# Half-depth block products in the up projection, and a down projection with the depth as its outer loop

## The chip, the core and the metric

The kernel runs on one core of one Trainium2 chip. The metric is device time in microseconds from the first to the last instruction of one execution, in float32. TensorE (PE) multiplies a 128x128 stationary block with up to 512 moving columns and adds up in PSUM, which has eight banks of 128x512 float32 here; VectorE (DVE), ScalarE (ACT) and GpSimd (POOL) do the elementwise work on PSUM and SBUF (POOL on SBUF alone); every DMA is issued from SyncE's queue (SP).

## What is computed

One layer of a hybrid decoder: a token mixer, a cross-attention and a gated ConvFFN, each between two RMS norms and added to the residual. Only the ConvFFN and its last norm change:

```python
def conv_ffn(h, w_up, conv_w, conv_b, w_down):      # h (1024, 1024), w_up (1024, 5632), w_down (2816, 1024)
    a = causal_depthwise_conv(h @ w_up, conv_w, conv_b)   # output t reads t-2, t-1, t
    val, gate = jnp.split(a, 2, axis=-1)
    return (val * jax.nn.gelu(gate)) @ w_down

h = rmsnorm(x, g_ffn_pre)
x = x + rmsnorm(conv_ffn(h, ...), g_ffn_post)
```

## The kernel before

**Numbers.** Every float32 operand of a large product is held as a pair: `hi`, rounded by an ACT copy to the format that PE takes at full rate, and `lo`, the rest, from a DVE subtraction (`split`, L213 and L214). `mm3` (L193 to L195) makes a product of three matmuls for each 128-deep step: hi*hi, hi*lo, lo*hi.

**Layout.** Activations stand transposed: channels in partitions, tokens in the free axis, in two halves `h` of 512 tokens. The 5632 up channels are 44 blocks of 128; block i and block i+22 are the value and the gate of pair i, so there are 22 pairs. `xg[h][k]` is the input of half h in depth step k (of 8).

**Weights.** `Stream` (L53) holds one list of weight tiles of 128x512 in the order of use. A tile is loaded (SP, into one of 4 `raw` slots), split by ACT (L95) and DVE (L98; some tiles in `ON_POOL` go to POOL), and kept as a pair in 13 `w` slots. `pump`, called by `tick` once or twice in a product, keeps the splits `W_AHEAD` = 6 tiles ahead of use. `tick` also moves on the `sides`: generators such as `post` and `finish`, whose instructions are woven into the products.

**ConvFFN.** `up_block(i, q, h)` is one block of one half: 8 depth steps, 24 matmuls of 512 columns, two weight tiles. Then the convolution: ACT writes tap 2 and the bias (L1174), DVE adds the two shifted taps (L1177, L1178), and two short DVE operations carry the edge from half 0 to half 1 (L1181, L1182). For a gate, ACT applies GELU (L1186), POOL multiplies (L1188), and the product is split into `f_hl`. The first `LEAD` = 5 pairs are done for all of half 0 and then for all of half 1, since half 1's input comes from `post2[1]`, the norms after attention, which runs beside half 0's blocks (L684 to L707) and is emitted to its end before half 1's blocks begin.

**Down.** The 22 pairs are in six groups (`GROUPS`). After the first pair of a group, `down` of the group before it takes eight output blocks and both halves: 3 or 4 depth steps a product, evicted and added on DVE to 16 `ya` tiles (L1207). The last group is done in `quarters` for half 1: twice eight products of 256 columns, with the end norm of the first 256 tokens beside the products of the second.

**Order.** A planner (`schedule_with_timeline_sim=True`) simulates the program when it is built and lays down the order of each engine's instructions; at run time each engine takes its own in that order, waiting on semaphores. `pin` keeps the order as written (used in the second quarter).

Of the kernel before, what the change touches and what calls it, by code (L numbers as in the profile page):

```python
# [22 lines left out]
P = 128  # L23
# [8 lines left out]
GROUPS = (4, 4, 4, 3, 3, 4)  # L32
LEAD = 5
FILL = 3
B_FIRST = 1

W_AHEAD = 6
ON_POOL = ((4, 16, 1), (164, 184, 2))
# [8 lines left out]
TAIL_R = 1  # L47
TAIL_B = 3
# [4 lines left out]
SLOTS_3 = {"f": 19, "t": 6, "rs": 4}  # L53
BANKS = {"acc": 4, "sx": 3, "st": 1}
DOWN = [(h, 0, 512, b) for b in range(8) for h in range(2)]
LAST_A = [(0, 0, 512, b) for b in range(8)]


class Stream:
# [13 lines left out]
    def add(self, ap):  # L73
        self.items.append(ap)
        return len(self.items) - 1

    def load_to(self, n):
        n = min(n, len(self.items), self.done + SLOTS["raw"])
        while self.loaded < n:
            ap = self.items[self.loaded]  # L80
            t = self.k.slot("raw")
            w = ap.shape[1] * ap.shape[2]
            self.k.nc.sync.dma_start(t[:, :w].rearrange("p (a b) -> p a b", b=ap.shape[2]), ap)
            self.raw[self.loaded] = (t, w)
            self.loaded += 1

    def split_to(self, n):
        nc = self.k.nc
        n = min(n, len(self.items))
        while self.done < n:  # L90
            self.load_to(self.done + 1)
            i = self.done
            t, w = self.raw.pop(i)
            hi, lo = self.k.pair(self.tag.get(i, "w"))
            nc.scalar.copy(hi[:, :w], t[:, :w])  # L95
            eng = "g" if any(a <= i < b and i % m == 0 for a, b, m in ON_POOL) else "v"
            e = nc.vector if eng == "v" else nc.gpsimd
            e.tensor_tensor(lo[:, :w], t[:, :w], hi[:, :w], ALU.subtract)  # L98
            self.hl[i] = (hi, lo)
            self.done += 1  # L100
            self.load_to(self.done + SLOTS["raw"])

    def pump(self, limit=1):
        self.split_to(min(self.pos + self.ahead, self.done + limit))
        self.load_to(self.done + SLOTS["raw"])
# [7 lines left out]
class Builder:  # L113
# [74 lines left out]
    def mm3(self, ps, parts, ticks=2, first=True, last=True):  # L188
# [3 lines left out]
        for i, (lh, ll, rh, rl) in enumerate(parts):  # L192
            self.pin(nc.tensor.matmul(ps, lhsT=lh, rhs=rh, start=first and i == 0, stop=False))  # L193
            self.pin(nc.tensor.matmul(ps, lhsT=lh, rhs=rl, start=False, stop=False))  # L194
            self.pin(nc.tensor.matmul(ps, lhsT=ll, rhs=rh, start=False, stop=last and i == n - 1))  # L195
# [518 lines left out]
    def finish(self, m, acc, h, x2d):  # L714
# [3 lines left out]
        for i in range(KT):  # L718
            t = self.slot("f")
# [20 lines left out]
    def run(self):  # L740
        with ExitStack() as es:
# [15 lines left out]
            self.shut(p)  # L757

    def prepare(self, cp, dp):
# [23 lines left out]
        self.pairs = []  # L783
        p0 = 0
        for n in GROUPS:
            self.pairs.append(list(range(p0, p0 + n)))
            p0 += n
        ids["up"], ids["dn"] = {}, {}
        for h in range(2):
            for i in range(LEAD):  # L790
                for q in range(2):
                    ids["up"][i, q, h] = add("w_up", i + 22 * q)
        for gi, gp in enumerate(self.pairs):
            for j, i in enumerate(gp):
                if i >= LEAD:
                    for q in range(2):
                        ids["up"][i, q, 0] = ids["up"][i, q, 1] = add("w_up", i + 22 * q)
                if j == 0 and gi:
                    self.add_down(gi - 1)
        for j, i in enumerate(gp):  # L800
            for q in range(2):
                ids["up"][i, q, 1] = add("w_up", i + 22 * q)
            if j == B_FIRST - 1:
                self.add_down(gi)
# [34 lines left out]
        self.x2d = halves("x2d", 8)  # L839
        self.xg = [[], []]  # L840
# [3 lines left out]

    def add_down(self, gi):
        k0, n = self.pairs[gi][0], len(self.pairs[gi])
        for b in range(8):
            i = self.ids["dn"][gi, b] = self.w.add(self.a["w_down"][b][:, k0:k0 + n])
            if gi == len(self.pairs) - 1:
                self.w.tag[i] = "b"  # L850
# [164 lines left out]
    def attention(self):  # L1015
# [108 lines left out]
        m2 = [[None] * 8, [None] * 8]  # L1124
# [32 lines left out]

    def ffn(self):
        nc, w, ids, pairs = self.nc, self.w, self.ids, self.pairs
        v, g = nc.vector, nc.gpsimd  # L1160
        conv = self.conv
        nc.sync.dma_start(conv, self.a["conv"])
        edge = self.tiny([P, 44, 2], "edge", 1)
        self.side(self.post2[1], POST_2B)
        val, f_hl, ya = {}, {}, {}

        def up_block(i, q, h):
            blk = i + 22 * q
# [3 lines left out]
            t = self.slot("t")  # L1172
            cw = lambda j: conv[:, blk, j:j + 1]
            nc.scalar.activation(t, ps, AF.Identity, bias=cw(3), scale=cw(2))  # L1174
            if h == 0:
                nc.scalar.copy(edge[:, blk], ps[:, 510:512])  # L1176
            v.scalar_tensor_tensor(t[:, 1:512], ps[:, 0:511], cw(1), t[:, 1:512], ALU.mult, ALU.add)  # L1177
            v.scalar_tensor_tensor(t[:, 2:512], ps[:, 0:510], cw(0), t[:, 2:512], ALU.mult, ALU.add)  # L1178
            if h == 1:
                hl = edge[:, blk]  # L1180
                v.scalar_tensor_tensor(t[:, 0:1], hl[:, 1:2], cw(1), t[:, 0:1], ALU.mult, ALU.add)  # L1181
                v.scalar_tensor_tensor(t[:, 0:2], hl[:, 0:2], cw(0), t[:, 0:2], ALU.mult, ALU.add)  # L1182
            if q == 0:
                val[i, h] = t
                return
            nc.scalar.activation(t, t, AF.Gelu_apprx_tanh)  # L1186
            f = val.pop((i, h))
            g.tensor_tensor(f, f, t, ALU.mult)  # L1188
            hl = f_hl[i, h] = self.pair("f")
            self.split(*hl, f)  # L1190

        def down(gi, sections=DOWN):
            gp = pairs[gi]
            n = len(gp)
            last = gi == len(pairs) - 1
            for h, c0, c1, b in sections:
                c = slice(c0, c1)
                hi, lo = w.get(ids["dn"][gi, b])
                ps = self.bank()[:, :c1 - c0]
                self.mm3(ps, [(hi[:, P * j:P * j + P], lo[:, P * j:P * j + P], *(t[:, c] for t in f_hl[gp[j], h]))  # L1200
                              for j in range(n)], ticks=1)
                if gi == 0:
                    ya[b, h] = self.slot("m")
                    nc.scalar.copy(ya[b, h], ps)
                    continue
                t = ya[b, h][:, c]
                v.tensor_tensor(t, t, ps, ALU.add)  # L1207
                if last:
                    if b == 0:
                        sq = self.slot("ac")  # L1210
                    self.sumsq(t, sq, b == 0)
                    if b == 7:
                        self.side(self.finish([ya[i, h] for i in range(8)], sq, h, self.x2d), 1)

        def quarters(gi):

            gp = pairs[gi]
            n = len(gp)
            wide = lambda x: x[:, :256].unsqueeze(1).to_broadcast([P, 2, 256])
            prev = None  # L1220

            def add(x):
                acc, sq, e = x
                self.pin(e.tensor_tensor(acc, acc, sq, ALU.add))

            for c0 in (0, 256):
                c = slice(c0, c0 + 256)
                self.pinned = c0 > 0
                acc = self.slot("ac")[:, :256]
                mg, res = [], []  # L1230
                steps = iter(())
                for b in range(8):
                    hi, lo = w.get(ids["dn"][gi, b])
                    ps = self.bank()[:, :256]
                    self.mm3(ps, [(hi[:, P * j:P * j + P], lo[:, P * j:P * j + P], *(t[:, c] for t in f_hl[gp[j], 1]))
                                  for j in range(n)], ticks=0)
                    if b % 2 == 0:
                        mg.append(self.slot("rs" if c0 else "t", shape=[P, 2, 256]))
                        res.append(self.slot("f", shape=[P, 2, 256]))
                    nc.sync.dma_start(res[-1][:, b % 2], self.x2d[b][1][:, c])  # L1240
                    t = ya[b, 1][:, c]
                    self.pin(v.tensor_tensor(t, t, ps, ALU.add))
                    sq = acc if b == 0 else self.slot("sq")[:, :256]
                    nc.scalar.activation(sq, t, AF.Square)
                    if b > 1:
                        add(late)
                    late = acc, sq, g if c0 == 0 and b < 6 else v
                    nc.scalar.activation(mg[-1][:, b % 2], t, AF.Identity, scale=self.gain["g_ffn_post"][:, b:b + 1])
                    if prev:
                        if b == TAIL_R:  # L1250
                            r = self.rms(prev[0], 2)
                        if b == TAIL_B:
# [119 lines left out]
```

## Time and profile before

| | |
|---|---|
| median of 3 runs | 1438.21 us (1436.39 to 1438.9) |
| the profiled execution, its time | 1437.53 us |
| its span, first to last instruction | 1435.8 us |
| mean granted TensorE clock | 0.972 |
| instructions | 18623, of which 6712 matmuls |
| DMA | 144.38 MB, 33.4% of 16 engines' span |

The page of the profile gives each engine's busy time and the mean duration of each group of instructions. Matmuls overlap: the duration of one is longer than the distance to the next, so what one more or less is worth is read from the distance of their starts in the timeline. Row counts of the matmuls may lack a few per cent.

### The profile page before, as it was taken

What the parts mean: (1) busy time and instruction counts of PE and PEld (TensorE: products, weight loads), DVE (VectorE), ACT (ScalarE), POOL (GpSimd) and SP (SyncE); (2) the same over time, 40 slices, a digit from 0 to 9 for tenths busy, and PEclk for the clock granted to TensorE, in tenths of its full rate; (3) what the DMA queues carried; (4) which work ended last, traced back from release to release, by engine and by line L of the source; (5) the groups of instructions that cost most, each with busy time, mean ns of one, the idle gap of its engine ahead of it and who ended that gap; (6) DMA issues with size and microseconds to landing.
All of it is one profiled execution on the core that took longest, in us unless ns stands there. A gap on an engine that the chain in (4) does not pass through costs nothing.

```text
span 1435.8 us, 18623 instructions
## 1 busy us (share of the span) xinstructions
PE 1361.4 (95%) x6712; PEld 1150.9 (80%) x6712; DVE 879.1 (61%) x1532; ACT 545.7 (38%) x1032; POOL 397.3 (28%) x336
## 2 busy tenths in 40 slices
PE   9799898799989998899989999999999999999996
PEld 7689887688868886788778888888888888888885
DVE  7968798874485558856787424444443454455576
ACT  7224321355454444445354423322331231324433
POOL 1675526832280027304641001000110010100313
PEclk9899999799999999999989999999999999999998
DMA  9653335264262135523424211111111112123441
GB/s 319 181 155 106 87 101 149 82 204 139 89 197 75 52 97 168 161 66 99 127 91 117 74 45 52 44 52 52 45 52 47 43 44 59 42 62 110 140 139 60
DMA packets 102268, 144.38 MB, mean 101 GB/s; under 512 B 28320, under 2 KB 39712, under 8 KB 102176
## 3 DMA queue, kind: packets, MB, share of 16 engines
q1 hardware_dynamic: 102176, 143.19, 33.4%
q8 instruction: 53, 0.87, 0.3%
q14 instruction: 39, 0.32, 0.1%
HBM read 119.71 MB, written 19.25 MB: 97 GB/s over the span
## 4 chain that ended last, share of the span: by engine, by line
PE 71%; DVE 13%; DMA 5%; issue 5%; POOL 4%; ACT 1%; SPq 1%; DVEq 0%; POOLq 0%; ACTq 0%
PE acc L194 22%; PE acc L195 22%; PE acc L193 22%; DVE w L98 2%; POOL ac L671 1%; DMA raw<-in_w_q 1%; DVE m L684 1%; DMA rs<-in_xT 1%; PE st L266 1%; PE sx L195 1%; DMA x<-x 1%; PE sx L193 1%; DVE x L558 1%; PE sx L194 1%; PE st L239 1%
## 5 line engine op out<-in xcount | busy, mean ns | idle before, releaser
L194 PE MATMUL acc<-b,w 128*128 128x512 f32 x1200 | 472.5, 394 | 7.3 <-DVE b L691 4.4
L193 PE MATMUL acc<-b,w 128*128 128x512 f32 x1200 | 473.0, 395 | 2.2 <-DVE t L1178 2.2
L195 PE MATMUL acc<-b,w 128*128 128x512 f32 x1200 | 471.8, 393 | 1.2 <-DVE w L98 1.2
L98 DVE TENSOR_TENSOR w<-raw,w 128x512 fp32r<-128x512 f32 (+1 forms) x302 | 249.5, 831 | 272.8 <-PE acc L194 201.0
L95 ACT CAST w<-raw 128x512 fp32r<-128x512 f32 (+1 forms) x324 | 198.7, 615 | 307.2 <-PE acc L195 248.5
L194 PEld LDWEIGHTS acc<-b,w 128*128 128x128 f32 x1200 | 228.3, 190 | 56.4 <-DVE b L691 6.3
L193 PEld LDWEIGHTS acc<-b,w 128*128 128x128 f32 x1200 | 228.3, 190 | 49.5 <-issue 2.8
L195 PEld LDWEIGHTS acc<-b,w 128*128 128x128 f32 x1200 | 227.7, 190 | 49.7 <-DVE w L98 2.7
L1188 POOL TENSOR_TENSOR t<-t,t 128x512 f32<-128x512 f32 x44 | 57.2, 1300 | 584.1 <-ACT t L1186 579.5
L671 POOL TENSOR_TENSOR ac<-ac,sq 128x512 f32<-128x512 f32 x49 | 72.2, 1482 | 192.3 <-ACT sq L670 148.5
L1177 DVE SCALAR_TENSOR_TENSOR t<-acc,conv,t 128x511 f32<-128x511 f32 x88 | 65.8, 748 | 85.7 <-ACT edge L1176 76.9
L1174 ACT ACTIVATE t<-acc,conv 128x512 f32<-128x512 f32 x88 | 68.5, 778 | 125.5 <-PE acc L195 125.4
L193 PE MATMUL acc<-f,w 128*128 128x512 f32 x288 | 112.0, 389 | 0.0
L194 PE MATMUL acc<-f,w 128*128 128x512 f32 x288 | 112.0, 389 | 0.0
L195 PE MATMUL acc<-f,w 128*128 128x512 f32 x288 | 112.0, 389 | 0.0
L1207 DVE TENSOR_TENSOR m<-m,acc 128x512 f32<-128x512 f32 x72 | 49.1, 684 | 44.8 <-PE acc L195 44.8
L1178 DVE SCALAR_TENSOR_TENSOR t<-acc,conv,t 128x510 f32<-128x510 f32 x88 | 65.5, 745 | 1.2
L685 POOL TENSOR_TENSOR m<-m,rs 128x512 f32<-128x512 f32 x32 | 52.4, 1647 | 50.0 <-DVE m L684 14.9
L193 PEld LDWEIGHTS acc<-f,w 128*128 128x128 f32 x288 | 54.1, 188 | 11.2
L194 PEld LDWEIGHTS acc<-f,w 128*128 128x128 f32 x288 | 54.1, 188 | 11.2
L195 PEld LDWEIGHTS acc<-f,w 128*128 128x128 f32 x288 | 54.1, 188 | 11.2
L670 ACT ACTIVATE sq<-m 128x512 f32<-128x512 f32 x63 | 39.5, 631 | 39.8 <-DVE ac L671 16.3
(314 smaller groups left out, 2019.0 us busy)
## 6 DMA issues: line engine op xcount, KB each, us to landing
raw<-in_w_up SPq DMA_DIRECT2D x124, 256.0 KB, 2.6
raw<-in_w_out SPq DMA_DIRECT2D x32, 256.0 KB, 2.6
raw<-in_w_q SPq DMA_DIRECT2D x32, 256.0 KB, 2.7
raw<-in_w_o SPq DMA_DIRECT2D x32, 256.0 KB, 2.6
raw<-in_w_down SPq DMA_DIRECT2D x32, 256.0 KB, 2.6
m<-in_xT SPq DMA_DIRECT2D x16, 256.0 KB, 5.2
x<-in_x SPq DMA_DIRECT2D x16, 256.0 KB, 5.2
x<-x SPq DMA_DIRECT2D x32, 128.0 KB, 2.4
```

What stands on the lines that cost most here:

```text
L95: nc.scalar.copy(hi[:, :w], t[:, :w])
L98: e.tensor_tensor(lo[:, :w], t[:, :w], hi[:, :w], ALU.subtract)
L193: self.pin(nc.tensor.matmul(ps, lhsT=lh, rhs=rh, start=first and i == 0, stop=False))
L194: self.pin(nc.tensor.matmul(ps, lhsT=lh, rhs=rl, start=False, stop=False))
L195: self.pin(nc.tensor.matmul(ps, lhsT=ll, rhs=rh, start=False, stop=last and i == n - 1))
L671: (e or nc.gpsimd).tensor_tensor(acc, acc, sq, ALU.add)
L685: g.tensor_tensor(x, x, rs, ALU.add)
L1174: nc.scalar.activation(t, ps, AF.Identity, bias=cw(3), scale=cw(2))
L1177: v.scalar_tensor_tensor(t[:, 1:512], ps[:, 0:511], cw(1), t[:, 1:512], ALU.mult, ALU.add)
L1178: v.scalar_tensor_tensor(t[:, 2:512], ps[:, 0:510], cw(0), t[:, 2:512], ALU.mult, ALU.add)
L1188: g.tensor_tensor(f, f, t, ALU.mult)
L1207: v.tensor_tensor(t, t, ps, ALU.add)
```

## The change

**Up projection.** Pairs 0 to 4 stay as they are. For each of pairs 5 to 21, value (row 1) and gate (row 2), the two depth halves, and the two token halves make a 2x2 by 2x2 block product, which took eight products of four depth steps. It is done in seven (Strassen's scheme, in Winograd's form), with four sums of weight blocks for each pair (`Stream.sums` and one line of `split_to`, all on POOL) and four sums of the input once (`t_sums`: 16 POOL operations and 16 splits, beside half 1's blocks of pairs 0 to 4). The seven weight blocks of a pair are split separately. The partial results are added up partly in the PSUM bank (a product goes on in a bank whose content has been copied out) and partly by three DVE additions. Up to four banks of a pair's results become the conv inputs, most of them now tiles in SBUF.

```diff
+TURN = ((1, "11"), (0, "22"), (0, "S4"), (1, "12"), (1, "S2"), (1, "S1"), (1, "S3"))
...
+    def sums(self, p):
+        g = self.k.nc.gpsimd
+        p["S1"] = self.k.slot("rs")
+        g.tensor_tensor(p["S1"], p["21"], p["22"], ALU.add)
+        p["S3"] = p["21"]
+        g.tensor_tensor(p["S3"], p["11"], p["21"], ALU.subtract)
+        p["S2"] = p["11"]
+        g.tensor_tensor(p["S2"], p["S1"], p["11"], ALU.subtract)
+        p["S4"] = p["12"]
...
+        for k in range(4):
+            a, b, c, d = x1[k], x1[k + 4], x0[k], x0[k + 4]
+            g.tensor_tensor(d, d, c, ALU.subtract)
+            g.tensor_tensor(c, c, a, ALU.subtract)
+            yield
+            put(3, d, v)
...
+        for n in range(LEAD - 1, NP):
+            for d, name in TURN:
...
+                if name == "11":
+                    s["A"] = self.bank()
+                    product(i, name, s["A"], True)
+                    s["p1"] = self.slot("m")
+                    nc.scalar.copy(s["p1"], s["A"])
+                elif name == "12":
+                    B = self.bank()
+                    product(i, name, B, True)
+                    u = s["p1"]
+                    v.tensor_tensor(u, u, B, ALU.add)
+                    s["v1"] = self.slot("m")
+                    self.conv_main(s["v1"], u, i)
+                elif name == "S2":
+                    product(i, name, s["A"])
+                    s["u2"] = self.slot("m")
+                    nc.scalar.copy(s["u2"], s["A"])
+                elif name == "S1":
+                    s["E"] = self.bank("sx")
+                    product(i, name, s["E"], True)
+                elif name == "S3":
+                    product(i, name, s["A"])
+                    u = s["u3"] = self.slot("m")
+                    nc.scalar.copy(u, s["A"])
+                    v.tensor_tensor(u, u, s["E"], ALU.add)
+                    s["g0"] = self.slot("m")
+                    self.conv_main(s["g0"], u, i + NP)
+                elif name == "22":
+                    product(i, name, s["A"])
+                    s["g1"] = self.slot("m")
+                    self.conv_main(s["g1"], s["A"], i + NP)
...
+                elif name == "S4":
+                    product(i, name, s["E"])
+                    u = s["u2"]
+                    v.tensor_tensor(u, u, s["E"], ALU.add)
+                    s["v0"] = self.slot("m")
+                    self.conv_main(s["v0"], u, i)
```

Each `product` is 12 matmuls with one tick. `conv_main` and `conv_edge` are the convolution of before in functions of their own.

**Between.** The gated product is no longer split at once: `gated` stores it to HBM (`fd`), 44 tiles of 256 KB, and `get_f` loads each back later and splits it, `F_AHEAD` = 3 depth steps ahead of its use.

**Down projection.** `GROUPS`, `down` by groups and `quarters` go. For each half, `sweep` keeps seven output blocks in seven PSUM banks and runs through the 22 depth steps once; the eighth block follows alone (`last`), for half 1 in two parts of 256 columns. The down weights are loaded and split once for each half. For half 1's end, `done1` takes scale and square straight from the bank.

```diff
+        def sweep(h, done):
+            ps = [self.bank("acc" if b < 4 else "sx") for b in range(7)]
+            for k in range(NP):
+                get(h * NP + k + F_AHEAD)
+                hl = [w.get(i) for i in ids["dn"][h, k]]
+                for b in range(7):
+                    c = slice(b % 4 * P, b % 4 * P + P)
+                    hi, lo = hl[b // 4]
+                    self.mm3(ps[b], [(hi[:, c], lo[:, c], *f[h, k])], ticks=0, first=k == 0, last=k == NP - 1)
+                    if b in (3, 6):
+                        self.tick()
+                    if k == NP - 1:
+                        done(b, ps[b])
...
+        sweep(0, done0)
+        ps = self.bank("st")
+        last(0, ps, slice(0, HALF), steps0)
...
+        sweep(1, done1)
...
+        last(1, ps, quarters[0], lambda k: None)
...
+        last(1, ps, quarters[1], steps1)
```

The slots of the stage are dealt out anew (`T` 24 for the input sums, `t` 3 where there were 6, `rs` 2 or 4), the last group's up weights are no longer loaded twice, and `TAIL_R` and `TAIL_B`, the steps of the end at which the first quarter's norm is computed and spread, count depth steps (5 and 10) instead of output blocks.

More of the change, by code (lines that the diff above doesn't have):

```diff
@@ L92, in split_to @@
             i = self.done
-            t, w = self.raw.pop(i)
+            pair, name = self.items[i][1:]
+            if pair is None:
+                t, w = self.raw.pop(i)
+            else:
+                if name == "S2":
+                    self.sums(pair)
+                if name == "S1":
+                    nc.gpsimd.tensor_tensor(pair["S4"], pair["12"], pair["S2"], ALU.subtract)
+                t, w = pair[name], HALF
             hi, lo = self.k.pair(self.tag.get(i, "w"))
@@ L192, in mm3 @@
         for i, (lh, ll, rh, rl) in enumerate(parts):
-            self.pin(nc.tensor.matmul(ps, lhsT=lh, rhs=rh, start=first and i == 0, stop=False))
-            self.pin(nc.tensor.matmul(ps, lhsT=lh, rhs=rl, start=False, stop=False))
-            self.pin(nc.tensor.matmul(ps, lhsT=ll, rhs=rh, start=False, stop=last and i == n - 1))
+            for j, (x, y) in enumerate(((lh, rh), (lh, rl), (ll, rh))):
+                self.pin(nc.tensor.matmul(ps, lhsT=x, rhs=y, start=first and i + j == 0,
+                                          stop=last and i == n - 1 and j == 2, skip_group_check=go_on))
             if ticks and (i + 1) * ticks // n > i * ticks // n:
@@ L757, in run @@
             self.shut(p)
+            p = self.open(SLOTS_4)
+            self.down()
+            self.shut(p)
     def prepare(self, cp, dp):
@@ L782, in prepare @@
             ids["o2"][h] = [add("w_o", i) for i in range(8)]
[L783 to L788, printed above, removed]
+        ids["up"], ids["dn"], ids["d7"] = {}, {}, {}
         for h in range(2):
@@ L843, in prepare @@
         self.mix = {}
[L845 to L850, printed above, removed]
     def mixers(self):
@@ L1171, in up_block @@
             self.mm3(ps, [(*part(k), *self.xg[h][k]) for k in range(8)])
-            t = self.slot("t")
-            cw = lambda j: conv[:, blk, j:j + 1]
-            nc.scalar.activation(t, ps, AF.Identity, bias=cw(3), scale=cw(2))
+            t = self.slot("t" if h else "T")
+            self.conv_main(t, ps, i + NP * q)
+            e = edge[:, 2 * i + q]
             if h == 0:
-                nc.scalar.copy(edge[:, blk], ps[:, 510:512])
-            v.scalar_tensor_tensor(t[:, 1:512], ps[:, 0:511], cw(1), t[:, 1:512], ALU.mult, ALU.add)
@@ L1178, in up_block @@
[L1178 to L1204, printed above, removed]
-                    continue
[L1206 to L1252, printed above, removed]
-                            bc = self.bcast(r, 2)[1]
-                            for i in (3, 2):
-                                self.drain(self.finish_pair(prev[1][i], prev[2][i], wide(bc), i, 1, 0, g))
-                            steps = self.chain(*(self.finish_pair(prev[1][i], prev[2][i], wide(bc), i, 1, 0, v)
-                                                 for i in (0, 1)))
-                        if TAIL_B < b < 7:
-                            next(steps, None)
-                add(late)
-                prev = acc, mg, res
-            self.drain(steps)
-            r = self.rms(acc, 2)
-            ps, bc = self.bcast(r, 2)
-            self.drain(self.finish_pair(mg[3], res[3], wide(bc), 3, 1, 256, g))
-            gens = [self.finish_pair(mg[i], res[i], wide(ps), i, 1, 256, v) for i in range(3)]
-            for i in (0, 1, 0, 2, 1, 2):
-                next(gens[i], None)
@@ L1287, in ffn @@
-        late = [(1, 0, 512, b) for b in range(8 - FILL, 8)]
-        for h in range(2):
-            for j, i in enumerate(gp):
-                for q in range(2):
-                    up_block(i, q, h)
-                if h == 0 and j == 0:
-                    down(gi - 1, [x for x in DOWN if x not in late])
-                if h == 1 and j == B_FIRST - 1:
-                    down(gi, LAST_A)
-            self.xg[h] = []
-        down(gi - 1, late)
+                nc.scalar.copy(e, ps[:, 510:512])
+            else:
+                self.conv_edge(t, e, i + NP * q)
@@ new lines, in up_block @@
+            return t
+        for h in range(2):
+            if h:
+                self.drain(self.post2[1])
+                sums = self.side(self.t_sums(), T_RATE)
+            for i in range(LEAD):
+                val = up_block(i, 0, h)
+                self.gated(i, h, val, up_block(i, 1, h))
+        self.drain(sums)
+        x0, x1 = self.xg
+        ops = {"11": x1[:4], "12": x1[4:], "S4": x0[4:], "22": self.T[4], "S1": self.T[1], "S2": self.T[2],
+               "S3": self.T[3]}
+        st = {i: {} for i in range(LEAD, NP)}
@@ new lines, in ffn, with product @@
+        self.f = {}
+        def product(i, name, ps, first=False):
+            part = self.blocks([ids["up"][i, name]])
+            self.mm3(ps, [(*part(k), *ops[name][k]) for k in range(4)], ticks=1, first=first, go_on=not first)
+        for n in range(LEAD - 1, NP):
+            for d, name in TURN:
+                i = n + d
+                if i not in st:
+                    continue
+                s = st[i]
+                if i == NP - 1 and name in F_FIRST:
+                    self.get_f(F_FIRST[name], "t")
+                if name == "11":
[28 more added lines that the diff above has]
+                    self.conv_main(s["g1"], s["A"], i + NP)
+                    self.conv_edge(s["g1"], s["u3"][:, 510:512], i + NP)
+                elif name == "S4":
[4 more added lines that the diff above has]
+                    self.conv_main(s["v0"], u, i)
+                    self.conv_edge(s["v1"], u[:, 510:512], i)
+                    self.gated(i, 0, s["v0"], s["g0"])
+                    self.gated(i, 1, s["v1"], s["g1"])
+                    st[i] = None
@@ L1298, in ffn, with steps1 @@
         for s in [s[0] for s in self.sides]:
             self.drain(s)
-        quarters(gi)
+        ps = self.bank()[:, :256]
+        last(1, ps, quarters[0], lambda k: None)
+        done1(7, ps, (0,))
+        self.pinned = True
+        out = []
+        st = {}
+        def steps1(k):
+            if k == TAIL_R:
+                st["r"] = self.rms(acc[:, quarters[0]], 2)
+            if k == TAIL_B:
+                bc = self.bcast(st["r"], 2)[1]
+                for i in (3, 2):
+                    self.drain(self.finish_pair(mg[0][i], res[0][i], wide(bc), i, 1, 0, g))
+                st["out"] = self.chain(*(self.finish_pair(mg[0][i], res[0][i], wide(bc), i, 1, 0, v) for i in (0, 1)))
+            if k > TAIL_B and k % 2:
+                next(st["out"], None)
@@ L1303 @@
+        ps = self.bank()[:, :256]
+        last(1, ps, quarters[1], steps1)
+        self.drain(st["out"])
+        done1(7, ps, (1,))
+        r = self.rms(acc[:, quarters[1]], 2)
+        ps, bc = self.bcast(r, 2)
+        self.drain(self.finish_pair(mg[1][3], res[1][3], wide(bc), 3, 1, 256, g))
+        gens = [self.finish_pair(mg[1][i], res[1][i], wide(ps), i, 1, 256, v) for i in range(3)]
+        for i in (0, 1, 0, 2, 1, 2):
+            next(gens[i], None)
 GAINS = ("g_mix_pre", "g_mix_post", "g_x_pre", "g_x_post", "g_mem", "g_ffn_pre", "g_ffn_post")
```

191 lines of the change are left out of this document (134 added, 57 removed).

## The prediction

> **What bounds the kernel now.** First the page: its busy table and the clock row of the 40 slices. Then the windows of the ConvFFN.
>
> ```profile
> PE 1361.4 (95%) x6712; PEld 1150.9 (80%) x6712; DVE 879.1 (61%) x1532; ACT 545.7 (38%) x1032; POOL 397.3 (28%) x336
> PEclk9899999799999999999989999999999999999998
> 750.00:806.00 56.00, 54.66 (x240) 44.96 (x241) 40.40 (x74) 25.14 (x43) 8.23 (x6) 1.00 0.37 103
> 806.00:1361.00 555.00, 555.00 (x2450) 459.73 (x2449) 243.71 (x405) 170.41 (x306) 50.33 (x39) 1.00 0.21 59
> 1361.00:1396.00 35.00, 34.73 (x161) 28.47 (x161) 28.48 (x62) 11.60 (x19) 3.85 (x3) 1.00 0.40 131
> 1396.00:1420.00 24.00, 23.89 (x200) 23.68 (x199) 13.67 (x35) 11.56 (x30) 8.91 (x9) 1.00 0.13 41
> 1420.00:1436.00 16.00, 1.80 (x8) 1.45 (x8) 10.09 (x25) 2.00 (x5) 3.53 (x3) 0.66 0.33 115
> ```
>
> From 806 to 1361 us PE has no idle time at the full clock, while DVE is busy 44% (243.71 of 555), ACT 31%, POOL 9%. This stretch holds nearly all the edited work: a matmul less there is time won, and an elementwise operation more is free until its engine fills up. What is a matmul worth? Not the 394 ns that the page gives as its mean: the timeline shows the distance of starts.
>
> ```profile
> 1150.02 0.39 PE L194 MATMUL acc<-b,w 128*128 128x512 f32 x1
> ...
> 1152.96 0.39 PE L195 MATMUL acc<-b,w 128*128 128x512 f32 x1
> ...
> 1400.86 0.28 PE L193 MATMUL acc<-f,b 128*128 128x256 f32 x1
> ...
> 1409.02 0.28 PE L195 MATMUL acc<-f,b 128*128 128x256 f32 x1
> ```
>
> 13 steps lie between the first two rows: 2.94 / 13 = 0.226 us for 512 columns (555 us / 2450 = 0.2265 agrees; I use that). 68 steps lie between the other two: 0.120 us for 256 columns.
>
> **The sum, part by part.** It is made against the profiled execution, 1437.53 us with a span of 1435.8; the median shown, 1438.21, is 0.7 us above it.
>
> *Matmuls of the up projection.* 17 pairs x 4 blocks x 24 = 1632 become 17 x 7 x 12 = 1428. 204 fewer x 0.2265 = **-46.2 us**. Had I used 394 ns it would have been 80.
>
> *Matmuls of the down projection.* Before: 18 pairs x 16 x 3 + 8 x 4 x 3 = 960 wide ones and 192 of 256 columns: 217.4 + 23.0 = 240.4 us. After: 2 x 7 x 22 x 3 + 66 = 990 and 132: 224.2 + 15.8 = 240.0. **-0.4 us.** The additions into `ya` that go stood beside a busy PE: worth nothing.
>
> *Does the elementwise work still fit?* A pair now lasts 7 x 12 x 0.2265 = 19.0 us on PE. What stands beside it:
>
> ```profile
> 936.30 0.69 DVE L98 TENSOR_TENSOR w<-raw,w 128x512 fp32r<-128x512 f32 x1 [2.08 <-ACT f L213]
> 936.91 0.69 DVE L214 TENSOR_TENSOR f<-t,f 128x512 fp32r<-128x512 f32 x1
> 937.51 0.74 DVE L1177 SCALAR_TENSOR_TENSOR t<-acc,conv,t 128x511 f32<-128x511 f32 x1
> 938.17 0.21 DVE L1181 SCALAR_TENSOR_TENSOR t<-edge,conv,t 128x1 f32<-128x1 f32 x1
> 938.30 0.74 DVE L1178 SCALAR_TENSOR_TENSOR t<-acc,conv,t 128x510 f32<-128x510 f32 x1
> ...
> L95 ACT CAST w<-raw 128x512 fp32r<-128x512 f32 x308 | 190.6, 620 | 300.8 <-PE acc L195 242.1 <-DMA raw<-in_w_k 10.3 <-DMA raw<-in_w_q 7.6
> L1174 ACT ACTIVATE t<-acc,conv 128x512 f32<-128x512 f32 x88 | 68.5, 778 | 125.5 <-PE acc L195 125.4
> L1186 ACT ACTIVATE t<-t 128x512 f32<-128x512 f32 x44 | 27.8, 631 | 53.0 <-DVE t L1182 25.7 <-DVE t L1178 25.0 <-DVE st_x L242 2.3
> L1204 ACT COPY m<-acc 128x512 f32<-128x512 f32 x16 | 9.4, 587 | 27.3 <-PE acc L195 27.3
> L1188 POOL TENSOR_TENSOR t<-t,t 128x512 f32<-128x512 f32 x44 | 57.2, 1300 | 584.1 <-ACT t L1186 579.5 <-PE st L266 4.6
> ...
> 750.86 1.63 POOL L214 TENSOR_TENSOR b<-m,b 128x512 fp32r<-128x512 f32 x1 [1.28 <-ACT b L213]
> 751.26 1.78 DVE L98 TENSOR_TENSOR w<-raw,w 128x512 fp32r<-128x512 f32 x1
> ```
>
> DVE back to back: a subtraction or addition every 0.61 us, a conv tap every 0.66, an edge 0.13. A pair has 7 lo-subtractions and 3 additions (6.1 us), 8 taps (5.3), 4 edges (about 0.7): 12.1 us of 19.0. ACT: 7 x 0.62 + 3 x 0.59 + 4 x 0.78 + 2 x 0.63 = 10.5. POOL: 4 sums and 2 gate products x 1.30 = 7.8; before, POOL was idle here for nine tenths. That is new, because the last two rows show what a POOL operation beside a DVE one costs: the subtraction took 1.78 us where it takes 0.69 alone, 1.09 more. Six a pair make at most 6.5 us, so DVE stands between 12.1 and 18.6 of 19.0. Two taps and the three additions have an operand in PSUM; a tap of that kind never stretched (736/750/753 in the view of its line):
>
> ```profile
> L1177 DVE SCALAR_TENSOR_TENSOR t<-acc,conv,t x88: 736/750/753, 686.2 to 1390.9; 128x511 f32<-128x511 f32 x88
> ```
>
> So I take about two thirds of it, 4.5: DVE at 16.6, 87%. It fits, with little air. The subtraction of 751.26 ended at 753.04, 0.55 us after the POOL operation (750.86 to 752.49), as if it had stood still till then; so the delay of one pairing may reach POOL's whole 1.30, and that is the first rival below. The Trainium skill (SBUF — State Buffer, section Who interferes with whom) has the same as a rule: a DVE instruction with two SBUF inputs and a GpSimd instruction that reads SBUF exclude each other for the whole instruction. By that rule, with every POOL operation paired, the sum would be the first rival's and not mine; these two rows agree with it.
>
> *New waits of PE inside a pair.* A bank is copied out by ACT before the next product goes on in it: p1 has three products of cover (8.2 us), u2 (S1 stands between) and u3 (11 of the next pair) one each, 2.72 us, for a copy of 0.59, by L1204's row; E waits for a DVE addition with two products of cover. Queued behind a waiting PE instruction is everything that PE has; behind a late ACT copy stand the weight casts, which are 6 tiles (16 us) ahead. The cover is lost when ACT's queue is over 2 us late, as when it waits for DVE ahead of a copy. I put 4 us on 17 pairs (bounds 0 and, as a rival, over 1 us a pair): the nearest row is 806 to 1361, where the same kind of evictions cost PE nothing, but with DVE at 44%.
>
> *The first five pairs.* PE lost time here before, to DVE:
>
> ```profile
> 708.92 1.70 DVE f L214
> ...
> 750.73 0.60 DVE f L214
> ...
> 717.18 0.47 PE L193 MATMUL acc<-b,w 128*128 128x512 f32 x1 [2.24 <-DVE t L1178]
> ...
> 718.79 0.63 PE L193 MATMUL acc<-b,w 128*128 128x512 f32 x1
> ...
> 721.35 0.63 PE L193 MATMUL acc<-b,w 128*128 128x512 f32 x1
> ...
> 750.79 0.50 PE L194 MATMUL acc<-b,w 128*128 128x512 f32 x1 [2.27 <-DVE b L214]
> ```
>
> The chain of waits (first two rows) has f splits in it, 1.70 and 0.60 us; the timeline (the others) has PE's idle times behind DVE. The f splits leave: **-2 us** (bounds -4 and 0). Then, beside half 1's blocks (54.4 us of PE), come 16 input sums on POOL (21 to 28 us) and 16 splits on DVE (16 x 0.61 = 9.8). Window 750 to 806 has DVE at 40.4 of 56 us; less some 4 of f splits, with 9.8 and 16 x 1.09 = 17 of mutual delay, it comes to 46 to 63. Six weight tiles and four banks (16 us each) buffer some of the excess: **+3 us** (bounds 0 and 12).
>
> *f by way of HBM, and loads.* 44 stores, 44 loads, 48 more tiles of down weights. In the up stage a pair moves 4 + 2 tiles of 256 KB in 19 us (83 GB/s); in the sweep a depth step of 21 x 0.2265 = 4.76 us takes 192 + 2 x 256 KB, 151 GB/s.
>
> ```profile
> 1300.00:1361.00 61.00, 61.00 (x271) 50.53 (x270) 33.92 (x53) 28.48 (x52) 14.18 (x11) 1.00 0.43 133
> raw<-in_w_down SPq DMA_DIRECT2D x32, 256.0 KB, 2.6
> ```
>
> 133 GB/s went beside a full PE at a DMA share of 0.43, and a tile lands in 2.6 us, against leads of 9 us and more. A store waits on SP for POOL, with weight loads behind it; these run far enough ahead. DVE and ACT have three splits each in these 4.76 us, under 2.1 and 1.9. Cost 0, hidden by PE; if the cover went, the sweeps would stretch by their own length's share. *Stage changes*: seven banks must be free at once, behind DVE's last additions and taps; between the sweeps the eighth block (66 x 0.2265 = 15 us) covers seven evictions of 0.59 and, for the square, by GELU's row, 0.63 on ACT. **+2 us** (0 to 5).
>
> *The end.*
>
> ```profile
> 1419.61 0.28 PE L195 MATMUL acc<-f,b 128*128 128x256 f32 x1
> ...
> 1422.88 0.42 ACT L1244 ACTIVATE sq<-m 128x256 f32<-128x256 f32 x1 [0.45 <-DVE m L1242]
> ...
> 1423.20 0.49 ACT L1248 ACTIVATE rs<-m,gains 128x256 f32<-128x256 f32 x1
> ...
> 1423.33 0.42 DVE L1224 TENSOR_TENSOR ac<-ac,sq 128x256 f32<-128x256 f32 x1 [0.21 <-ACT sq L1244]
> ...
> 1423.81 0.61 PE L239 MATMUL st<-ones,ac 128*128 128x1 f32 x4 [3.92 <-DVE ac L1224]
> ```
>
> 4.0 us from the last product to the norm's matmul, as DVE was behind. Without the additions it is scale, square, add (0.49 + 0.42 + 0.42, some 1.8 with waits): -2; the first quarter's norm, now 1.8 us of products ahead of its spread, may hold PE for 1. **-1 us** (-2 to +1).
>
> Sum: -46.2 - 0.4 + 4 - 2 + 3 + 2 - 1 = -40.6; 1437.5 - 40.6 = **1396.9 us**.
>
> **The rivals.**
> - *DVE full.* If each POOL operation stops DVE for its whole 1.30: 12.1 + 7.8 = 19.9 a pair, 0.9 over PE; with head-of-line waits 1 to 2. 17 x 0.9 = 15 at least, and the sums of the input at their bound (+9): 1397 + 24 = **1421 us**. For it: 1.78 against 0.69. Against: the operations with a PSUM operand, and that POOL must wait as often as DVE.
> - *Slower than before: PE held in every pair.* If ACT's copy of u2 or u3 is late by more than its 2.1 us of slack because ACT waits for DVE, PE idles twice a pair, and after idles of about 2 us the trace shows matmuls 0.43 apart (718.79 to 721.35) instead of 0.227: 7 of them, 1.4 us. 2 x (1 + 1.4) x 17 = 82 on top of the 4: 1397 + 78 = **1475 us**. It turns slower at 2.4 us a pair beyond my sum (40.6 / 17). Against it: the order is laid out with one product of cover everywhere.
> - *No stalls.* The elementwise work hides entirely: -46.2 - 0.4 - 4 - 2 = **1385 us**.
> - *Not 204 fewer.* The counts follow from the loops; I give it nothing.
>
> **How the numbers follow.** Forecast 1389 to 1408: 0.62. DVE full, 1408 to 1434: 0.20. No stalls, below 1389: 0.08. Slower: 0.08, and 0.02 for within 0.2% (2.9 us, about what a measurement of this kernel can tell). Range 1386 to 1426: it leaves out half of the no-stall case, the end of the DVE case and all of the slower one. Faster 0.90, same 0.02, slower 0.08.
>
> **What would show it.** Right: 6478 or so matmuls, a pair every 19 to 19.5 us with PE full, DVE at 80 to 92% there, sweep steps of 4.76 us, 12 to 14 us after the last product. Wrong: PE idle before S3 or 22 on ACT, or on the DVE subtraction of a weight tile; PEclk under 9 in the pairs' slices; sweep steps longer than 5 us (DMA). The whole falls if DVE's queue takes over 21 us a pair.

## The result, and the profile after

The changed kernel takes 1400.91 us (median of 4 runs, 1399.46 to 1404.58) against 1438.16 before: a ratio of 0.9747, with a 95% interval of 0.9724 to 0.9769. The profiled execution took 1399.61 us, 37.9 less than the profiled one of before; the forecast was 1396.9.

First the page of the changed kernel, its busy table and clock row, and then its windows (the columns are those of before: length, busy us of PE, PEld, DVE, ACT and POOL with instruction counts, clock, DMA share, GB/s):

```profile
PE 1320.2 (94%) x6478; PEld 1117.3 (80%) x6478; DVE 987.6 (71%) x1597; ACT 617.8 (44%) x1137; POOL 534.1 (38%) x415
...
PEclk9899999889999999999998999999999999999998
```

```profile
710.00:735.00 25.00, 20.47 (x88) 16.71 (x87) 20.52 (x32) 12.17 (x27) 14.18 (x10) 0.93 0.65 211
735.00:755.00 20.00, 12.07 (x49) 9.61 (x48) 18.34 (x15) 9.46 (x16) 16.90 (x11) 0.78 0.29 93
755.00:778.00 23.00, 19.93 (x85) 16.12 (x83) 23.00 (x29) 13.59 (x27) 11.72 (x8) 0.95 0.24 73
778.00:821.00 43.00, 42.79 (x177) 35.20 (x178) 30.56 (x57) 18.52 (x30) 17.83 (x13) 0.93 0.39 115
821.00:1138.00 317.00, 317.00 (x1401) 262.56 (x1400) 250.05 (x361) 160.74 (x265) 137.64 (x93) 1.00 0.26 81
1138.00:1157.00 19.00, 19.00 (x85) 15.74 (x84) 16.08 (x27) 12.57 (x23) 4.27 (x2) 1.00 0.87 280
1157.00:1240.00 83.00, 83.00 (x368) 68.75 (x367) 32.66 (x55) 30.11 (x54) 0.00 (x0) 1.00 0.53 163
```

Read it from below. The sweep (1157 to 1240) and the stage change ahead of it (1138 to 1157) keep PE full. So do the pairs in seven products (821 to 1138): not one idle microsecond in 317, with DVE busy 79% (250.05) and POOL 43%. The time that PE loses in the up projection lies higher, between 710 and 778 us, in the first five pairs. The chain of waits gives the step of the two new stages; a line is start, length, engine, output and count:

```profile
916.68 2.72 PE sx L226 x12
...
935.72 2.72 PE sx L226 x12
...
1161.25 2.72 PE acc L226 x12
1166.01 2.72 PE acc L226 x12
```

A pair comes every 19.04 us and a depth step of the sweep every 4.76, both exactly the product counts times the 0.2265 us of before. Where PE waited instead is in its timeline (the brackets give the idle time before a line and what ended it), with POOL's and DVE's beside it:

```profile
725.10 1.18 PE L271 MATMUL st<-ones,ac 128*128 128x1 f32 x8 [4.53 <-DVE ac L703]
...
750.53 5.92 PE L226 MATMUL acc<-b,w 128*128 128x512 f32 x13 [7.93 <-DVE b L246]
...
778.21 2.04 PE L226 MATMUL acc<-b,w 128*128 128x512 f32 x4 [3.28 <-DVE t L1194]
...
738.09 5.13 POOL L1216 TENSOR_TENSOR m<-m,m 128x512 f32<-128x512 f32 x3 [2.48 <-DVE m L739]
743.18 1.71 POOL L246 TENSOR_TENSOR b<-m,b 128x512 fp32r<-128x512 f32 x1
744.85 1.72 POOL L1216 TENSOR_TENSOR m<-m,m 128x512 f32<-128x512 f32 x1
746.53 3.40 POOL L246 TENSOR_TENSOR b<-m,b 128x512 fp32r<-128x512 f32 x2
...
737.26 11.53 DVE L739 SCALAR_TENSOR_TENSOR m<-m,gains,st 128x512 f32<-128x512 f32 x8
```

L1216 is the second input sum of `t_sums`, L739 the last scaling of half 1's norm, L246 the splits (`b` is the input of half 1's first block). In the program the sums are written after `post2[1]` is drained; the planner has put them on POOL as soon as a scaled tile is there, four of them ahead of the last splits. DVE's eight scalings, beside them, take 11.53 us; before the change they took 10.05, in its timeline:

```profile
740.08 10.05 DVE L707 SCALAR_TENSOR_TENSOR m<-m,gains,st 128x512 f32<-128x512 f32 x8 [1.38 <-ACT st L269]
```

PE waits 7.93 us for `b`, and the 13 matmuls after it stand 0.44 us apart (5.92 less one length of 0.63, by 12), half the clock. At 778.21 it waits 3.28 us more, for an operation of the convolution that DVE does late. The wait of 4.53 us ahead of the norm isn't new: before, PE lost 4.42 us in that stretch (25 - 20.58 in its windows, shown further on).

### The profile page after: what moved, and what is told of

The parts are those of the page before. It is cut to its first block, busy times and chain, and to the rows that moved or that the text cites. A ratio compares the mean times of both kernels' runs of the same rounds, so it can differ in the third digit from the quotient of the medians.

```text
span 1397.9 us, 18936 instructions
## 1 busy us (share of the span) xinstructions
PE 1320.2 (94%) x6478; PEld 1117.3 (80%) x6478; DVE 987.6 (71%) x1597; ACT 617.8 (44%) x1137; POOL 534.1 (38%) x415
## 4 chain that ended last, share of the span: by engine, by line
PE 68%; DVE 14%; issue 5%; DMA 5%; POOL 4%; ACT 2%; SPq 1%; DVEq 0%; POOLq 0%; ACTq 0%
PE acc L226 48%; PE sx L226 15%; DVE w L130 2%; PE st L226 2%; DVE m L716 1%; DMA raw<-in_w_q 1%; POOL m L717 1%; POOL ac L703 1%; DMA k<-gd 1%; PE st L298 1%; PE st L271 1%; DVE m L739 1%; DVE b L246 1%; DVE T L246 1%; ACT w L127 1%
## 5 line engine op out<-in xcount | busy, mean ns | idle before, releaser
L226 PE MATMUL acc<-b,w 128*128 128x512 f32 (+1 forms) x3060 | 727.4, 393 | 16.0 <-DVE b L246 7.9
L226 PEld LDWEIGHTS acc<-b,w 128*128 128x128 f32 x3060 | 575.8, 192 | 136.2 <-DVE b L246 8.4
L127 ACT CAST w<-raw 128x512 fp32r<-128x512 f32 x334 | 201.7, 606 | 255.2 <-PE acc L226 132.6
L226 PE MATMUL sx<-b,w 128*128 128x512 f32 x588 | 142.2, 389 | 0.0
L226 PEld LDWEIGHTS sx<-b,w 128*128 128x128 f32 x588 | 110.4, 188 | 22.9
L226 PE MATMUL acc<-T,w 128*128 128x512 f32 x408 | 98.0, 389 | 0.0
L226 PEld LDWEIGHTS acc<-T,w 128*128 128x128 f32 x408 | 76.6, 188 | 15.9
L1199 POOL TENSOR_TENSOR m<-m,m 128x512 f32<-128x512 f32 x34 | 59.0, 1736 | 67.4 <-DVE m L1189 33.6
L1188 DVE SCALAR_TENSOR_TENSOR m<-m,conv,m 128x511 f32<-128x511 f32 x51 | 41.5, 814 | 14.7 <-ACT m L1187 14.7
L226 PE MATMUL acc<-w,b 128*128 128x256 f32 x384 | 51.4, 292 | 0.0
L1189 DVE SCALAR_TENSOR_TENSOR m<-m,conv,m 128x510 f32<-128x510 f32 x51 | 50.9, 1004 | 0.0
```

Source lines behind the costliest of these rows:

```text
L226: self.pin(nc.tensor.matmul(ps, lhsT=x, rhs=y, start=first and i + j == 0, stop=last and i == n - 1 and j == 2, skip_group_check=go_on))
L1188: v.scalar_tensor_tensor(t[:, 1:512], src[:, 0:511], self.cw(blk, 1), t[:, 1:512], ALU.mult, ALU.add)
L1189: v.scalar_tensor_tensor(t[:, 2:512], src[:, 0:510], self.cw(blk, 0), t[:, 2:512], ALU.mult, ALU.add)
L1199: nc.gpsimd.tensor_tensor(val, val, gate, ALU.mult)
```

## The experiments

Nine kernels were run. All are edits of the changed kernel, and each time stands beside runs of the kernel before on the same chip; the ratio is to that kernel. Theory A, formed from the lines above: the input sums cost by their place and by their pairing with DVE. Theory B: DVE is simply full in that stretch.

**1. No input sums.**

```diff
-            g.tensor_tensor(d, d, c, ALU.subtract)
-            g.tensor_tensor(c, c, a, ALU.subtract)
             yield
             put(3, d, v)
-            g.tensor_tensor(a, d, a, ALU.add)
             yield
             put(1, c, v)
-            g.tensor_tensor(b, b, a, ALU.subtract)
```

> Leaves out the 16 additions of input tiles on POOL; the 16 splits stay, of unsummed tiles. Theory A (the planner puts these POOL operations ahead of the last four splits of half 1's input, and PE waits 7.9 us there): most of the wait goes, 1391 to 1395 us. Theory B (DVE is simply full there, with the 16 splits and the taps): the sums' place is harmless, 1398 to 1401 us.

1391.65 us (1388.89 to 1392.89), ratio 0.9673 [0.9657, 0.9688]: 9.3 us less than the changed kernel. This is theory A's forecast. The kernel leaves out only the additions; the 16 splits stayed, so it isn't their number on DVE.

**2. The sums in their written order on POOL.** Each of the four lines is wrapped so that the planner can't draw it ahead:

```diff
+        keep = self.tc.keep_in_program_order
...
-            g.tensor_tensor(c, c, a, ALU.subtract)
+            keep(g.tensor_tensor(c, c, a, ALU.subtract))
```

> The same 16 POOL additions, but kept on POOL behind everything written before them, so behind half 1's last splits. Theory A: the 7.9 us before half 1's first block shrink to the 2.3 us of before, 1392 to 1397 us. Theory B (the amount of work, not its place): the wait only moves to half 1's blocks, 1399 to 1402 us.

1395.66 us (1392.46 to 1398.5), ratio 0.9703 [0.9683, 0.9722]. About half of what leaving them out gives. The timeline of this run:

```profile
750.09 40.23 PE L226 MATMUL acc<-b,w 128*128 128x512 f32 x169 [3.87 <-DVE b L246]
```

The wait before the first block fell from 7.93 to 3.87 us (the 2.3 of before weren't reached), and after it 169 matmuls follow without idle time. But the windows show PE at 41.79 of 45 us further on, from 780 to 825, with POOL at 31.50 and DVE at 42.23: part of the cost had only moved, as theory B has it. The next 25 us, in the second row, have PE busy throughout, but at a clock of 0.91:

```profile
780.00:825.00 45.00, 41.79 (x181) 33.95 (x180) 42.23 (x60) 20.86 (x36) 31.50 (x20) 0.97 0.37 111
825.00:850.00 25.00, 25.00 (x103) 20.43 (x102) 16.69 (x24) 9.53 (x16) 9.60 (x7) 0.91 0.23 66
```

The wait in between is for a weight split that DVE does late (timeline):

```profile
823.43 2.93 PE L226 MATMUL acc<-b,w 128*128 128x512 f32 x6 [3.21 <-DVE w L130]
```

**3. The sums on DVE, in written order.** As in 2, with `v` in place of `g`:

```diff
-            g.tensor_tensor(c, c, a, ALU.subtract)
+            keep(v.tensor_tensor(c, c, a, ALU.subtract))
```

> The 16 additions on DVE instead of POOL, behind what is written before them. If pairing of POOL and DVE operations is what costs (16 x 1.09 us), DVE gains more than the 16 x 0.61 = 9.8 us that it takes on: 1390 to 1396 us and at or below the run with the sums on POOL in order. If DVE's amount of work bounds this stretch: 1400 to 1408 us.

1389.85 us (1388.0 to 1391.89), ratio 0.9663 [0.9648, 0.9679]. DVE took on 16 operations in its fullest stretch, and the median is 5.8 us below that of experiment 2, whose interval of the ratio lies wholly above this one. The windows:

```profile
755.00:780.00 25.00, 25.00 (x112) 20.72 (x111) 25.00 (x46) 15.80 (x27) 5.20 (x2) 1.00 0.42 116
780.00:825.00 45.00, 45.00 (x200) 37.27 (x199) 40.55 (x58) 21.36 (x36) 23.45 (x15) 1.00 0.33 106
825.00:850.00 25.00, 25.00 (x112) 20.71 (x111) 21.18 (x30) 12.33 (x21) 10.58 (x8) 1.00 0.30 85
```

PE is full from 755 on, though DVE is busy the whole 25 us of the first line. The wait of 3.21 us is gone, and from 780 to 850 us 28 matmuls more are done (312 against 284), 6.3 us at 0.2265 each. The two profiled executions are 9.5 us apart (1398.5, the slowest of experiment 2, and 1389.01); 2.5 of these were there already at half 1's first block (750.09 and 747.55). So theory B alone falls: with 16 operations more, DVE was no longer late.

The pairing isn't all of it. These are the windows from half 1's first block to the end of the split that PE waited for in experiment 2: that run first, then the same work here.

```profile
750.09:823.40 73.31, 70.13 (x300) 57.22 (x300) 66.94 (x91) 35.11 (x62) 51.70 (x32) 0.97 0.35 106
```

```profile
747.55:816.80 69.25, 69.25 (x298) 57.24 (x299) 67.66 (x107) 35.33 (x61) 27.74 (x16) 0.98 0.37 112
```

With the 16 additions on it (107 instructions against 91) DVE is busy only 0.72 us longer. At 0.61 us each, the additions on POOL thus cost DVE some 9 us by pairing, 0.57 each: as much as doing them itself, and half of the 1.09 that the forecast has for each. The 4.1 us by which experiment 2 is longer come from idle time of DVE: 6.4 us against 1.6. In experiment 2's timeline DVE waits longest for a cast by ACT, and ACT for POOL's first sum:

```profile
760.33 0.62 ACT L245 CAST T<-m 128x512 fp32r<-128x512 f32 x1 [2.40 <-POOL m L1216]
```

```profile
760.98 1.23 DVE L246 TENSOR_TENSOR T<-m,T 128x512 fp32r<-128x512 f32 x1 [3.08 <-ACT T L245]
```

So two things fit together: the pairing fills DVE as much as the work itself would, and whatever waits for the sums, which take POOL 1.28 to 1.81 us each, waits longer. No run takes one away without the other.

**4. Without the seven products: the new down projection alone.**

```diff
-        for n in range(LEAD - 1, NP):
-            for d, name in TURN:
...
+        for i in range(LEAD, NP):
+            t = {}
+            for q in range(2):
+                for h in range(2):
+                    t[q, h] = up_block(i, q, h, "m")
+            for h in range(2):
+                self.gated(i, h, t[0, h], t[1, h])
```

> No seven-product scheme and no input sums: pairs 5 to 21 in whole products of 24 matmuls, gated product by way of HBM, down projection as a stage of its own as in the changed kernel. If the down stage is worth nothing (-0.4 us by count): 1400.9 + 46.2 - 10 (the wait for the input sums) = 1437 us, 1434 to 1440. If the new stage itself loses or gains time, outside of that by as much.

1436.71 us (10 runs, 1432.98 to 1438.51), ratio 0.9988 [0.9976, 1.0]. The new stage, its trips through HBM and its second load of the down weights are worth little, as the count said (-0.4 us): by the interval between nothing and 3.5 us. The whole gain is the 204 matmuls, less the price of the input sums: 1436.71 - 46.2 = 1390.5, which is the time of experiments 1 and 3.

**5. The weight sums of a pair on DVE.**

```diff
-        g.tensor_tensor(p["S1"], p["21"], p["22"], ALU.add)
+        self.k.nc.vector.tensor_tensor(p["S1"], p["21"], p["22"], ALU.add)
```

and so for the other three.

> The changed kernel, with the four weight sums of a pair on DVE instead of POOL. If a pair is PE's with room on DVE (15.0 us busy of 19.0): DVE takes on 4 x 0.61 = 2.4 us and loses most of its 2.9 us of mutual delay; no stall, 1397 to 1403 us, DVE at 14 to 16 us a pair. If DVE's queue has no room for work in its order: PE stalls of about 1 us a pair, 1415 to 1420 us.

1401.14 us (1400.67 to 1404.33), ratio 0.9743 [0.9725, 0.976]: no difference. Windows of the pairs, the changed kernel's first and then this run's:

```profile
850.00:1130.00 280.00, 280.00 (x1237) 231.94 (x1236) 224.91 (x328) 147.28 (x242) 123.95 (x84) 1.00 0.26 80
```

```profile
850.00:1130.00 280.00, 280.00 (x1237) 231.91 (x1236) 249.90 (x382) 143.95 (x237) 46.84 (x29) 1.00 0.27 80
```

280 us are 14.7 pairs. DVE went from 15.3 to 17.0 us a pair, a little over what was expected, so here the pairing had cost it only some 0.7 us for four sums (2.4 added, 1.7 seen). 89% on DVE still hides behind PE.

**6. Six more POOL operations a pair.**

```diff
-        g.tensor_tensor(p["S1"], p["21"], p["22"], ALU.add)
+        for _ in range(7):
+            g.tensor_tensor(p["S1"], p["21"], p["22"], ALU.add)
```

> The changed kernel, with one of a pair's weight sums done seven times on POOL: six POOL operations more a pair, twelve in all. If each stops DVE by the 1.09 us of the prediction (or POOL's whole 1.3): DVE would need 21 to 23 us of 19.0, so 2.5 to 4 us a pair, 1440 to 1465 us. If DVE loses only the 0.48 us for each POOL operation that the changed kernel's pairs show (2.9 us for six): DVE at 17.9 us, no or little stall, 1400 to 1410 us.

1469.24 us (1466.5 to 1475.43), ratio 1.0223 [1.0192, 1.0255]: slower than before the change. 68.3 us more than the changed kernel, 4.0 a pair, just above the dearer forecast. Its windows, its groups on DVE and a line of PE's timeline:

```profile
850.00:1130.00 280.00, 243.28 (x973) 192.55 (x972) 262.10 (x256) 112.87 (x188) 219.64 (x144) 0.93 0.22 67
```

```profile
L1189 DVE SCALAR_TENSOR_TENSOR m<-m,conv,m 128x511 f32<-128x511 f32 x36 | 53.1, 1476 | 8.0 <-ACT m L1188 8.0
...
L1189 DVE SCALAR_TENSOR_TENSOR m<-acc,conv,m 128x511 f32<-128x511 f32 x11 | 8.2, 747 | 3.6 <-ACT m L1188 3.6
```

```profile
908.69 4.63 PE L227 MATMUL sx<-T,w 128*128 128x512 f32 x10 [4.11 <-DVE w L131]
```

Only POOL got more work, and DVE is what fills up: it is busy 262.1 of 280 us. A pair takes 24.0 us in most of this stretch (the starts of DVE's addition behind S3 in the timeline), so DVE is busy 22.5 us a pair against 15.3, or 1.2 more for each operation added. The tap with both operands in SBUF takes 1476 ns on average, the same tap on a PSUM operand 747, as ever. The Trainium skill (SBUF — State Buffer, section Who interferes with whom) draws the line in the same place: a DVE instruction with two SBUF inputs excludes a GpSimd instruction that reads SBUF, one with at most one SBUF input, outside its 2-port perf modes, doesn't; these two rows agree. PE then waits for a weight split, up to 4.11 us, and its clock falls to 0.93 on average. This is the first rival of the prediction, and the point from which it decides: between 17.0 us of DVE a pair (experiment 5, no loss) and 22.5.

**7. A copy without cover.** The product that goes on in the bank just copied comes next to it:

```diff
-TURN = ((1, "11"), (0, "22"), (0, "S4"), (1, "12"), (1, "S2"), (1, "S1"), (1, "S3"))
+TURN = ((0, "22"), (0, "S4"), (1, "11"), (1, "12"), (1, "S2"), (1, "S1"), (1, "S3"))
```

> The changed kernel with the products of a pair in an order in which the product that goes on in the copied bank (22) comes right behind the one before it (S3), without the product of the next pair between them. If a copy not covered costs PE what the slower rival says (1 us of waiting and 1.4 us at half the clock in each pair): 17 x 2.4 = 41, about 1440 us. If it costs only the copy, its hand-over and no clock: 0.5 to 1.2 us a pair, 1408 to 1422 us. If the planner fills the gap: 1400 to 1404 us.

1418.21 us (1416.21 to 1418.8), ratio 0.986 [0.9844, 0.9876]: 17.3 us more, 1.0 a pair. The timeline, two pairs apart from one another by one period:

```profile
917.01 3.47 PE L226 MATMUL acc<-b,w 128*128 128x512 f32 x14 [0.68 <-ACT m L1299]
...
937.02 3.47 PE L226 MATMUL acc<-b,w 128*128 128x512 f32 x14 [0.68 <-ACT m L1299]
```

A pair takes 20.01 us instead of 19.04, with 0.68 us of plain idle time in it, and the granted clock in the pairs stays at 1.00. So the stall that a lost cover makes here costs 1.0 us and no clock, where the slower rival had 2.4 for each, 1.4 of it at half the clock. The rival took that clock from idle times of about 2 us, which no pair has in this run. Even with one copy uncovered in every pair the kernel stays faster than before.

**8 and 9. The end, and the splits of half 1.** In the changed kernel's end the norm's first matmul waited again 3.80 us, as before the change (3.92). Its timeline:

```profile
1380.77 0.88 PE L226 MATMUL acc<-f,w 128*128 128x256 f32 x6
1381.13 1.71 POOL L765 TENSOR_TENSOR m<-m,st 128x512 f32<-128x512 f32 x1
1381.65 1.75 DVE L765 TENSOR_TENSOR m<-m,st 128x512 f32<-128x512 f32 x1
...
1382.93 1.59 POOL L767 TENSOR_TENSOR m<-m,rs 128x512 f32<-128x512 f32 x1
1383.43 1.63 DVE L767 TENSOR_TENSOR m<-m,rs 128x512 f32<-128x512 f32 x1
1384.98 0.41 DVE L1398 TENSOR_TENSOR ac<-ac,sq 128x256 f32<-128x256 f32 x1
...
1385.45 1.01 PE L271 MATMUL st<-ones,ac 128*128 128x1 f32 x4 [3.80 <-DVE ac L1398]
```

The last addition (L1398) stands behind the first quarter's final operations, each at 1.6 to 1.75 us since POOL does the same kind at the same time. So one of DVE's two groups was given to POOL, on top of experiment 3 (8), and then also half 1's splits all to DVE (9):

```diff
-                for i in (3, 2):
+                for i in (3, 2, 1):
...
-                st["out"] = self.chain(*(self.finish_pair(mg[0][i], res[0][i], wide(bc), i, 1, 0, v) for i in (0, 1)))
+                st["out"] = self.finish_pair(mg[0][0], res[0][0], wide(bc), 0, 1, 0, v)
```

```diff
-                self.split(*hl, x, g if i % 2 else v)
+                self.split(*hl, x, v if h or i % 2 == 0 else g)
```

> As the run with the input sums on DVE in order, and in the end three of the first quarter's four groups on POOL and one on DVE (two and two before), so that DVE's last addition for the norm isn't queued behind them. If that queue is what holds the 3.8 us from the last product to the norm: it falls to about 1.5, 1387 to 1388.5 us. If ACT's square is what comes late: unchanged, 1390 us, or up to 2 us longer where POOL becomes the last.

> As the run before, and all eight splits of half 1's input on DVE (four were on POOL). If the wait of 3.9 us before half 1's first block is the pairing of POOL's four splits with DVE's: 1.5 to 2.5 us less than the run before. If DVE's amount of work there sets it: 0 to 1.5 us longer than the run before.

Run 8: 1390.59 us (1389.02 to 1391.32), ratio 0.9681 [0.9666, 0.9695]; no gain over experiment 3 (0.9663 [0.9648, 0.9679]). The wait did fall to 1.53 us (first row), but the time came back one step later, in the few operations on 128x2 that turn the sum into the norm (L256, L263). Run 8's timeline, and POOL's at that time:

```profile
1375.40 0.61 PE L271 MATMUL st<-ones,ac 128*128 128x1 f32 x4 [1.53 <-DVE ac L1399]
1376.52 1.18 DVE L256 TENSOR_TENSOR rs_t<-rs_y 128x2 f32<-128x2 f32 x1
1377.73 0.16 DVE L262 SCALAR_TENSOR_TENSOR rs_t<-rs_t,st_x 128x2 f32<-128x2 f32 x1
1377.93 1.11 DVE L263 SCALAR_TENSOR_TENSOR rs_y<-rs_t,rs_y 128x2 f32<-128x2 f32 x1
```

```profile
1376.42 1.26 POOL L765 TENSOR_TENSOR m<-m,st 128x512 f32<-128x512 f32 x1
1377.76 1.26 POOL L767 TENSOR_TENSOR m<-m,rs 128x512 f32<-128x512 f32 x1
```

An operation of 0.16 us takes 1.1 when it meets a POOL operation: two of them give 2.0 of the 2.3 us back (PE's next wait is 4.36 us, and 2.31 in experiment 3, where these operations take 0.16 each). Run 9: 1389.29 us (1386.93 to 1391.27), ratio 0.9671 [0.9651, 0.969]. The wait before half 1's first block fell to 1.36 us, in its timeline:

```profile
748.04 12.33 PE L226 MATMUL acc<-b,w 128*128 128x512 f32 x53 [1.36 <-DVE b L246]
```

Yet the gain over run 8 is within the spread of either; it isn't shown. The versions 3 and 9 are both some 11 us faster than the changed kernel and can't be told apart.

## Why the prediction held, and where it was off

The steps, predicted and measured, between the two profiled executions. The measured length of the first five pairs is what is left of the 37.9 us when the others are taken out.

| step | predicted | measured |
|---|---|---|
| up matmuls, 204 fewer | -46.2 | -46.2 (x6478, distance unchanged) |
| down matmuls | -0.4 | -0.4 (the stage as a whole: experiment 4) |
| waits inside 17 pairs | +4 | 0 |
| first five pairs: f splits gone, input sums | -2 + 3 | +10.6 |
| DMA, stage changes | 0 + 2 | 0 |
| end | -1 | +0.3 |
| ahead of the ConvFFN | none | -2.2 |
| sum | -40.6 | -37.9 |

**The matmul's worth** was right, and it decided the case: the distance of starts, 0.2265 us, and not the 394 ns of the groups, which would have promised 80 us.

**DVE's room in a pair** was right in kind and a little dear. 15.0 us a pair (250.05 of 317) against the 16.6 forecast, and 79%, just under the 80 to 92% that was to show it: six POOL operations cost DVE 2.9 us and not 4.5. By experiment 5 the four weight sums are only some 0.7 of that, so the rest falls to the two gate products. The additions with an operand in PSUM keep their 0.68 us in the pairs. Where POOL leaves fewer gaps an operation costs more: 1.2 in experiment 6, between the forecast's 1.09 and the rival's 1.30.

**New waits in a pair** were put at 4 us and were none. The product of cover was enough; without it a wait costs 1.0 us a pair (experiment 7).

**The step that failed** is "beside half 1's blocks come 16 input sums": +3 us forecast, +10.6 for the stretch with the f splits' gain in it, at the edge of the bounds that it was given (0 to 12). It took the order of the program for the order on the chip. The planner drew the sums forward, onto POOL ahead of the last splits of the norm, where they held both engines on which half 1's first block waits. By experiments 1 to 3 the sums cost some 9 us where they are, about 5 of it by their place, and the rest by being POOL's: done on DVE, they cost nothing that the times show. The mutual delay itself, for which the forecast allowed up to 17 us, is some 9 in experiment 2. In the windows of the changed kernel PE was idle for 15.7 us from 710 to 821 us. Before the change it was 7.2, all of it here (25 - 20.58 and 20 - 17.18):

```profile
712.00:737.00 25.00, 20.58 (x71) 16.14 (x71) 20.14 (x36) 12.13 (x24) 10.78 (x7) 0.80 0.49 147
737.00:757.00 20.00, 17.18 (x79) 13.71 (x78) 18.43 (x20) 11.10 (x23) 9.89 (x6) 1.00 0.19 52
```

That is 8.5 of the 10.6; the rest is put down to matmuls at a lower clock, which wasn't tried alone. The f splits' -2 wasn't measured alone; in experiment 4, where they are gone and the sums as well, the whole kernel gains 1.3 us by the medians, at most 3.5 by the interval.

**The end** was forecast to be shorter by the additions that go, with 12 to 14 us after the last product; 16.5 were seen (from the last start at some 1381.4, by the first row of experiment 8, to the span's end). These two forecasts don't fit one another: 16.2 us lay behind the last product before (1419.61 to 1435.8), so a gain of 1 leaves 15.2. The estimate counted ACT's and DVE's operations of the last tile, but not what is queued on DVE ahead of them.

**Ahead of the ConvFFN** the changed kernel was 2.2 us earlier: the norm's spread begins at 695.16 us in the timeline of before and at 692.96 in that of after:

```profile
695.16 1.05 PE L266 MATMUL st<-ident,rs_y 128*128 128x128 f32 x8
```

```profile
692.96 1.05 PE L298 MATMUL st<-ident,rs_y 128*128 128x128 f32 x8
```

Nothing was edited there; the planner's order and the loads differ. Other variants had it between 692.9 and 696.2. Its cause wasn't tried.

Of the rivals, "DVE full" didn't come at this load and was reached with six more POOL operations a pair; "slower" had its stall at 2.4 us, where experiment 7 shows 1.0; "no stalls" was right about the pairs and failed in the first five.

## What to carry to other kernels

Price a product that is taken out by the distance of matmul starts in a full stretch, and then ask only whether the added elementwise work fits the other engines: 89% of DVE still hid here. Additions given to POOL aren't free for DVE when both read SBUF: beside a full DVE, 16 of them held it as long as doing them would (0.57 us each against 0.61), came later, and moving them onto DVE brought the median down by 5.8 us. When a planner lays out the order, look up where it puts new work that is ready early; a stretch that was tight before is the first place to look, and pinning the work behind what is urgent is cheap to try.

## What the runs showed of the hardware beyond what was expected

The pairing of DVE and POOL strikes tiny operations too: a 128x2 operation went from 0.16 to 1.18 us (experiment 8), so a chain of small steps next to POOL work is stretched far beyond its own length. And PE's clock doesn't react to every gap: idles of 0.68 us in each 20 us left it at 1.00 (experiment 7), while 7.93 us of idle time were followed by matmuls 0.44 us apart.
